# Six column tiles of the input projection in the loop over the cached keys, and two gathers of the cache at the head of the heads' stage

## The chip, the cores and the metric

The kernel runs on one core of a Trainium2 chip. The metric is the device time of one execution in microseconds (us), the median of several runs. The page and the trace shown here come from one more execution, taken with the hardware profiler.

## What is computed

One layer of a hybrid decoder, for a prompt of 512 tokens and for eight sample tokens, each with a cache of 4096 older tokens in 32 pages. All numbers are float32. Cut to what matters:

```python
D_MODEL, SEQ, DEC_BATCH, PAST_LEN, PAGE_SIZE = 1024, 512, 8, 4096, 128
KV_LORA, Q_LORA, MLA_HEADS, MLA_ROPE = 256, 384, 8, 32

z = rmsnorm(h, g_attn) @ w_in            # q|k|v 1536, a 8, b 8, gate z 512, latent q 384, latent kv 256, rotary key 32
q, k, v, g, beta = gdn_prep(causal_conv(ext, w_conv), a, b, a_log, dt_bias)   # conv of 4 taps, silu, l2norm of q and k
o_gdn = gdn_output(gdn_chunked(q, k, v, g, beta)[0], z, g_gdn_out)             # prompt; gdn_recurrent for the samples

q_nope, q_rope, ckv, kr = mla_project(qa, kva, cos, sin, ...)
o_mla = mla_prompt_attention(...)        # prompt: causal attention among its 512 tokens
# samples: every cached page is gathered by page_table, its keys expanded and normed per head
kn_p, v_p = mla_expand(ckv_pool[pages], w_kv_b, g_k_nope)
sc_p = scores(kn_p, kr_pool[pages])      # softmax over 4096 cached tokens and the new one

h = h + concat(o_gdn, o_mla) @ w_o
h = h + (silu(u @ w_ffn_gate) * (u @ w_ffn_up)) @ w_ffn_down        # u = rmsnorm(h, g_ffn)
h = h + (p @ w_ple_proj) * sigmoid(rmsnorm(h, g_ple) @ w_ple_gate)
```

## The kernel before

Every float32 operand of a large product is kept as two float32r parts, hi and lo, and a product is three matmuls, hi*hi, hi*lo and lo*hi. Of a weight, ScalarE (ACT) makes the hi part by a copy and GpSimd (POOL) the lo part by a subtraction (L122, L123). The 520 tokens lie on the free dimension in two halves of 260 columns.

The order of the instructions on each engine is made ahead of time by a scheduler from priorities and its own model of the engines; the program text gives the order in which things are offered to it, and the gathers are offered under a raised priority. On the chip each engine works through its row in order.

The stages are these. Up to 46 us the norm of the tokens and a token-major projection (latent q, latent kv, rotary key, a, b), and the row numbers idx of the gathers. From 46 to 222 us, called the stage of the heads here, two things run side by side. One is the feature-major input projection: 16 column tiles of 128 columns, in `order`, 48 matmuls each into a pair of PSUM banks (ps_in, L664). Tiles 0 to 3 are q, 4 to 7 k, 8 to 11 v, 12 to 15 the gate z. Behind each tile `conv_tail` scales its columns (ct), and for q, k and v makes the convolution (four steps on y by VectorE, DVE), the silu (th by ACT, then a product), four transposes (ps_n), copies and sums of squares; for z it makes the gate and stores it. The other is the generator `latent_heads`, one step (`next(side)`) per k tile: the heads of the latent attention, that is projections of keys, values and queries (ps_k, ps_v, ps_q; ps_q14 is the last one, of the samples in the second half of the heads), their norms (rq, an inverse root by DVE in small steps), the gains (qs and qn by POOL, L578), rotations (rope, L393 to L398), and last, for the samples, the absorbed queries (ps_qg, ps_qabs, ps_qr, tiles qs, sq, qah, bd) that the loop over the keys needs. Its memory is then closed and taken by the pools of the cache (`after_heads`).

The cache comes in 64 groups, eight for a sample, of 512 tokens each. A group is two gathers issued by POOL: raw (512 KB, the latents) and kr (64 KB, the rotary keys). Eleven raw places (NRAW) and twelve kr places (NKR) exist; a raw place comes free when the latents of a sample have been weighted (softmax_pv, `released`), eight groups at a time.

The loop over the cached keys has 256 key tiles of 128 tokens, two for each n. Per pair of key tiles there are four transposes (ps_cT by `latents_T`), a copy (cth) and a subtraction (ctl) for the two parts; per key tile 12 matmuls ps_K (L1368), squares by ACT (sqk), scores by ACT (S), sums by DVE (ssq), and norms, softmax and weighting now and then. After each key tile one step of `filler` is taken (`pace`): the delta rule of the prompt (0.6 of the steps) and the prompt's attention (0.4), then the splits for the output projection, which itself and the FFN follow. TensorE's work up to about 930 us belongs to this loop and its filler; the rest is output projection, FFN and layer embedding.

## Time and profile before

| | us |
|---|---|
| median of 3 runs | 1440.86 |
| lowest and highest run | 1436.94 and 1441.38 |
| span of the profiled execution | 1436.1 |
| TensorE busy in it | 1337.7 (93%) |
| VectorE / ScalarE / GpSimd busy | 849.3 / 572.5 / 642.8 |
| chain of waits: PE / DVE / DMA / another core or an unknown queue | 73% / 12% / 6% / 3% |

The span is the time from the first to the last instruction of the profiled execution; the runs are timed from outside. Busy times are sums of instruction durations. Matmuls overlap one another, so that two of them of 0.28 us each can start 0.12 us apart; rows of a timeline join instructions of one kind that follow each other (x2). PEclk is the clock that TensorE was granted, in parts of its full 2.4 GHz; 0.5 is 1.2 GHz.

### The profile page before, as it was taken

How to read it: one execution, taken by the hardware profiler on the slowest of the kernel's cores; microseconds unless marked ns; L12 is line 12 of the kernel's file. 1: busy time of each engine (PE TensorE's matmuls, PEld its weight loads, DVE VectorE, ACT ScalarE, POOL GpSimd, SP SyncE). 2: the span in 40 equal slices, each digit the busy share in tenths (PEclk: the TensorE clock that was granted, in tenths of full speed). 3: DMA queues.
4: the chain of work that ended last, by engine and by line, in shares of the span. 5: the costliest groups of instructions: out<-in, count | busy, mean ns of one | idle time of the engine just before them, and what ended most of it. 6: DMA issues, size and time to landing. Idle time of an engine off the chain costs nothing.

```text
span 1436.1 us, 27870 instructions
## 1 busy us (share of the span) xinstructions
PE 1337.7 (93%) x11100; PEld 1271.4 (89%) x11100; DVE 849.3 (59%) x1628; ACT 572.5 (40%) x1304; POOL 642.8 (45%) x794
## 2 busy tenths in 40 slices
PE   7998884997898999899999998999999999999998
PEld 6888873996897989799799797989999999999998
DVE  5589991676777765446456575447666665411164
ACT  5354311553464555454355465424222222222232
POOL 3224546354557884321321527336434443445531
PEclk9999987999899999999999999999999999999999
DMA  7434326113454233310400505133333333232331
GB/s 225 108 100 136 67 66 225 28 31 79 155 108 138 59 124 72 119 31 5 136 11 26 168 5 174 39 96 89 91 100 90 89 89 97 88 93 88 94 111 38
DMA packets 198148, 132.41 MB, mean 92 GB/s; under 512 B 65000, under 2 KB 183043, under 8 KB 198012
## 3 DMA queue, kind: packets, MB, share of 16 engines
q1 hardware_dynamic: 186756, 92.88, 24.0%
q0 software_dynamic: 11264, 37.76, 7.8%
q8 instruction: 88, 1.44, 0.4%
q14 instruction: 40, 0.33, 0.1%
HBM read 116.71 MB, written 14.00 MB: 91 GB/s over the span
## 4 chain that ended last, share of the span: by engine, by line
PE 73%; DVE 12%; DMA 6%; another core or an unknown queue 3%; POOL 2%; issue 2%; ACT 1%; SPq 1%; POOLq 0%; DVEq 0%; ACTq 0%
PE ps_K L1368 21%; PE ps_d L1503 9%; PE ps_u L1193 9%; PE ps_g L1193 8%; PE ps_cT L1313 3%; PE ps_pg L1193 3%; PE ps_in L664 2%; DVE y L636 2%; PE ps_wom L1464 1%; PE ps_natA L320 1%; DMA db<-fac_d 1%; PE ps_pv L1284 1%; PE ps_wog L1223 1%; DMA raw<-in_cache_ckv_dram,idx 1%
## 5 line engine op out<-in xcount | busy, mean ns | idle before, releaser
L1368 PE MATMUL ps_K<-wkh,cth 128*128 128x260 f32 x1024 | 229.1, 305 | 8.5 <-issue 5.9
L1373 DVE TENSOR_REDUCE ssq<-sqk 128x8 f32<-128x512 f32 x256 | 174.0, 682 | 104.1 <-ACT sqk L1371 95.8
L1371 ACT ACTIVATE sqk<-ps_K 128x512 f32<-128x512 f32 x256 | 152.6, 597 | 180.0 <-PE ps_K L1368 160.3
L1368 PE MATMUL ps_K<-wkh,ctl 128*128 128x260 f32 x1024 | 214.6, 291 | 1.6 <-issue 1.6
L1368 PE MATMUL ps_K<-wkl,cth 128*128 128x260 f32 x1024 | 214.4, 290 | 0.8 <-issue 0.8
L1368 PEld LDWEIGHTS ps_K<-wkh,cth 128*128 128x128 f32 x1024 | 163.5, 196 | 14.6 <-issue 8.3
L1368 PEld LDWEIGHTS ps_K<-wkl,cth 128*128 128x128 f32 x1024 | 164.3, 195 | 1.9 <-issue 1.6
L1368 PEld LDWEIGHTS ps_K<-wkh,ctl 128*128 128x128 f32 x1024 | 162.6, 194 | 2.6 <-issue 2.0
L1319 DVE TENSOR_TENSOR ctl<-ps_cT,cth 128x512 fp32r<-128x512 f32 x128 | 87.5, 684 | 42.3 <-ACT cth L1318 36.0
L1313 PE MATMUL ps_cT<-cst,raw 128*128 128x128 f32 x512 | 81.8, 282 | 25.3 <-DVE ctl L1319 19.4
L1318 ACT ACTIVATE cth<-ps_cT 128x512 fp32r<-128x512 f32 x128 | 77.1, 603 | 69.0 <-PE ps_cT L1313 31.0
L608 POOL DMA_INDIRECT kr<-in_cache_krope_dram,idx x64 | 63.5, 993 | 83.0 <-PE ps_kr L1240 69.7
L1313 PEld LDWEIGHTS ps_cT<-cst,raw 128*128 128x128 f32 x512 | 60.9, 146 | 30.1 <-DVE ctl L1319 21.1
L123 POOL TENSOR_TENSOR wg_l<-wg_r,wg_h 128x1024 fp32r<-128x1024 f32 x22 | 53.6, 2436 | 71.6 <-ACT wg_h L122 71.6
L123 POOL TENSOR_TENSOR wu_l<-wu_r,wu_h 128x1024 fp32r<-128x1024 f32 x22 | 52.7, 2396 | 66.8 <-ACT wu_h L122 66.8
L123 POOL TENSOR_TENSOR wd_l<-wd_r,wd_h 128x1024 fp32r<-128x1024 f32 (+1 forms) x24 | 53.1, 2211 | 65.8 <-ACT wd_h L122 65.8
L123 POOL TENSOR_TENSOR win_l<-win_r,win_h 128x1024 fp32r<-128x1024 f32 x16 | 38.8, 2431 | 90.7 <-ACT win_h L122 90.7
L606 POOL DMA_INDIRECT raw<-in_cache_ckv_dram,idx x64 | 62.7, 979 | 33.1 <-issue 11.2
L1193 PE MATMUL ps_g<-ul,wg_h 128*128 128x260 f32 x352 | 71.0, 283 | 0.9 <-DVE ul L1432 0.7
L1193 PE MATMUL ps_u<-uh,wu_l 128*128 128x260 f32 x352 | 71.7, 283 | 0.0
L1193 PE MATMUL ps_u<-ul,wu_h 128*128 128x260 f32 x352 | 71.6, 283 | 0.0
L1193 PE MATMUL ps_u<-uh,wu_h 128*128 128x260 f32 x352 | 71.5, 283 | 0.0
(577 smaller groups left out, 3535.1 us busy)
## 6 DMA issues: line engine op xcount, KB each, us to landing
wg_r<-in_w_ffn_gate_dram SPq DMA_DIRECT2D x22, 512.0 KB
wu_r<-in_w_ffn_up_dram SPq DMA_DIRECT2D x22, 512.0 KB
win_r<-in_w_in_dram SPq DMA_DIRECT2D x16, 512.0 KB
wd_r<-in_w_ffn_down_dram SPq DMA_DIRECT2D x16, 512.0 KB
wpg_r<-in_w_ple_gate_dram SPq DMA_DIRECT2D x8, 512.0 KB
db<-fac_d SPq DMA_DIRECT2D x8, 384.0 KB
wd_r<-in_w_ffn_down_dram SPq DMA_DIRECT2D x8, 384.0 KB
xres<-xT_d SPq DMA_DIRECT2D x8, 260.0 KB
```

Source lines behind the costliest of these rows:

```text
L123: gp.tensor_tensor(out=lo, in0=raw, in1=f(hi), op=ALU.subtract)
L606: gp.indirect_dma_start(out=raws[G].rearrange("p t c -> p (t c)"), out_offset=None, in_=ckv_rows, in_offset=off)
L608: gp.indirect_dma_start(out=krs[G], out_offset=None, in_=kr_rows, in_offset=off)
L636: ve.scalar_tensor_tensor(out=y[:, s:], in0=ct[:, :SEQ - s], scalar=wtap(i, j), in1=y[:, s:], op0=ALU.mult, op1=ALU.add)
L1193: te.matmul(o[hf], w[a][:, k, :], mov[b][:, k, hf * HN:(hf + 1) * HN], start=k == 0 and (a, b) == (0, 0), stop=k == K - 1 and a == 1)
L1313: te.transpose(pt[:, (s * 2 + k) * P:(s * 2 + k + 1) * P], raw[:, (n % 2) * 2 + s, k * P:(k + 1) * P], ident)
L1318: sc.activation(hi, p4, AF.Copy)
L1319: ve.tensor_tensor(out=lo, in0=p4, in1=f(hi), op=ALU.subtract)
L1368: te.matmul(pk[:, hf, :260], x[:, s * 2 + k, :], y[:, k, hf, c0:c0 + 260], start=k == 0 and x is cur[0] and y is wkh, stop=k == 1 and x is ...
L1371: sc.activation(sq, pk[:, :, wo:wo + 256], AF.Square)
L1373: ve.tensor_reduce(out=ssq[:, i, :], in_=sq.rearrange("p f (h c) -> p (f h) c", h=4), axis=AX.X, op=ALU.add)
L1503: te.matmul(ps[:, hf, :HN], w[a][:, k, :], (fh, fl)[b][:, q0 + k, hf * HN:(hf + 1) * HN], start=q0 + k == 0 and a + b == 0, stop=q0 + k == ...
```

## The change

Six parts:

1. The loop of the stage of the heads keeps ten tiles, in the order 4, 12, 5, 13, 6, 14, 7, 15, 0, 1. Tiles 2, 3, 8, 9, 10 and 11 are made by a generator `project_qkv`, which stands at the head of the filler of the loop over the keys: four steps a tile (two halves of the columns, each in two halves of k), before the delta rule and the prompt's attention start.
2. Weights of the input projection come in pieces of four k tiles (256 KB) instead of eight (512 KB), with the splits half as long.
3. In the convolution, the copy of the last 11 columns and the first tap go from DVE to ACT, and its steps are taken between the matmuls of the next tile.
4. The gathers of the first two groups are issued at the head of the stage of the heads, into the place of oTm (free until the attention's outputs come) and into a tile kr_early; `after_heads` then issues eleven more. NKR goes from 12 to 11.
5. `pace` grows by 1.1 per key tile instead of 1.0.
6. The activations xh, xl and rb stay until `project_qkv` is done; the pool of the prompt's attention opens then. (Comments are gone as well, so that line numbers differ.)

```diff
-    NRAW, NKR = 11, 12
+    NRAW, NKR = 11, 11
+    early = 2
+    kr_early = dcp.tile([P, early, P], F32, name="kr_early")
     def gathers():
-        while len(raws) < min(NB * 8, NRAW + released[0]):
+        n = early if not dpool else min(NB * 8, NRAW + max(early, released[0]))
+        while len(raws) < n:
             G = len(raws)
-            raws[G] = dpool[1].tile([P, 4, 256], F32, tag="raw", name=f"raw{G}", bufs=NRAW)
-            krs[G] = dpool[1].tile([P, P], F32, tag="kr", name=f"kr{G}", bufs=NKR)
+            if G < early:
+                raws[G] = oTm.rearrange("p j t -> p (j t)")[:, G * 1024:(G + 1) * 1024].rearrange("p (t c) -> p t c", t=4)
+                krs[G] = kr_early[:, G, :]
+            else:
+                raws[G] = dpool[1].tile([P, 4, 256], F32, tag="raw", name=f"raw{G}", bufs=NRAW)
+                krs[G] = dpool[1].tile([P, P], F32, tag="kr", name=f"kr{G}", bufs=NKR)
...
+    def load_win(i):
+        c0 = i * P if i < 12 else CONV + 16 + (i - 12) * P
+        return [load_w(wk, w_in[q * 512:(q + 1) * 512, c0:c0 + P], 4, P, f"win{i}{q}", bufs_raw=2, bufs=3) for q in range(2)]
+
+    def project_qkv(tiles):
+        conv = iter(())
+        for i in tiles:
+            w = load_win(i)
+            ct = cv.tile([P, NT], F32, tag="ct", name=f"ct{i}")
+            for hf in range(2):
+                ps = psf(hf, f"ps_in{i}{hf}")
+                for q in range(2):
+                    for k in range(4):
+                        for a, b in ((0, 0), (0, 1), (1, 0)):
+                            te.matmul(ps[:, :HN], w[q][a][:, k, :], (xh, xl)[b][:, q * 4 + k, hf * HN:(hf + 1) * HN],
+                                      start=q + k + a + b == 0, stop=q + k == 4 and a == 1)
+                    if q:
+                        sl = slice(hf * HN, (hf + 1) * HN)
+                        ve.tensor_tensor(out=ct[:, sl], in0=ps[:, :HN], in1=rb[:, sl], op=ALU.mult)
+                    next(conv, None)
+                    yield
+            for _ in conv:
+                pass
+            conv = convolve(i, ct, psf(0, f"ps_n{i}"))
+        for _ in conv:
+            yield
+
+    def convolve(i, ct, pn):
+        sc.activation(ctail[:, i, :], ct[:, NT - 11:NT], AF.Copy)
         y = cv.tile([P, SEQ], F32, tag="y", name=f"y{i}")
-        ve.tensor_scalar(out=y, in0=ct[:, :SEQ], scalar1=wtap(i, 3), scalar2=None, op0=ALU.mult)
+        sc.activation(y, ct[:, :SEQ], AF.Copy, scale=wtap(i, 3))
...
+    gathers()
     side = latent_heads()
-    order = [4, 5, 6, 7, 0, 1, 2, 3, 8, 9, 12, 10, 13, 11, 14, 15]
-    for i in order:
+    conv = iter(())
+    for i in (4, 12, 5, 13, 6, 14, 7, 15, 0, 1):
...
     def mixers():
+        yield from project_qkv((2, 3, 8, 9, 10, 11))
+        px.close()
+        mhp.append(pmh.enter_context(pool("mh", 2, side="right")))
...
-            pace += 1.0
+            pace += 1.1
```

How this moves instructions is seen at three places. First TensorE at the last q projection. Before, after ps_q14 the next column tile goes on (ps_in12 here; ps_in of six tiles stand behind it in all):

```order
L561 MATMUL ps_q14_1595<-wqb1_h_1506,qaTl_1195 8x384
L561 MATMUL ps_q14_1595<-wqb1_l_1507,qaTh_1194 8x384
L644 MATMUL ps_n8_2006<-cst_133,y8_1998 128x128 x2
L664 MATMUL ps_in12_2090<-xh_95,win12_h_2086 128x260
L664 MATMUL ps_in12_2090<-xl_96,win12_h_2086 128x260 x2
L664 MATMUL ps_in12_2090<-xh_95,win12_l_2087 128x260 x2
```

In the changed kernel, at the same place:

```order
L561 MATMUL ps_q14_1609<-wqb1_h_1519,qaTl_1209 8x384
L561 MATMUL ps_q14_1609<-wqb1_l_1520,qaTh_1208 8x384
L675 MATMUL ps_n1_2029<-cst_133,kq_81 128x128 x4
L1358 MATMUL ps_cT0_2122<-cst_133,oTm_82 128x128 x4
L509 MATMUL ps_qg_1693<-cst_133,sq_1_1686 128x8 x4
L518 MATMUL ps_qabs0_1707<-qgT_1698,wkT_627 128x8 x8
L518 MATMUL ps_qabs1_1720<-qgT_1698,wkT_627 128x8 x8
L532 MATMUL ps_qr_1741<-cst_133,sq_2_1687 128x8 x4
L646 MATMUL ps_in20_2170<-xh_95,win20_h_2159 128x260
```

All ten tiles now stand ahead of ps_q14; behind it come the last transposes of tile 1, the first transposes of the cache, read from oTm, and the absorbed queries, and only then the first matmuls of tile 2 (ps_in20 and ps_in21 are its two halves). After 21 of those the second group of ps_qr follows.

Second TensorE where the loop over the keys begins (cT is the transposed cache, K00 and K01 the first two key tiles). Before:

```order
L664 MATMUL ps_in15_2417<-xh_95,win15_l_2414 128x260 x2
L1313 MATMUL ps_cT0_2499<-cst_133,raw0_1847 128x128 x4
L1368 MATMUL ps_K00_2517<-wkh_99,cth0_2504 128x260 x2
L1368 MATMUL ps_K00_2517<-wkl_100,cth0_2504 128x260 x2
L1368 MATMUL ps_K01_2534<-wkh_99,cth0_2504 128x260 x2
L1368 MATMUL ps_K01_2534<-wkl_100,cth0_2504 128x260 x2
L1313 MATMUL ps_cT1_2508<-cst_133,raw0_1847 128x128 x4
```

In the changed kernel (win30 and win31 are the two halves in k of the weights of tile 3):

```order
L646 MATMUL ps_in21_2239<-xh_95,win21_l_2166 128x260
L646 MATMUL ps_in30_2322<-xh_95,win30_h_2311 128x260
L646 MATMUL ps_in30_2322<-xl_96,win30_h_2311 128x260
L646 MATMUL ps_in30_2322<-xh_95,win30_l_2312 128x260
L1416 MATMUL ps_K00_2140<-wkh_99,cth0_2127 128x260 x2
L1416 MATMUL ps_K00_2140<-wkl_100,cth0_2127 128x260 x2
L1416 MATMUL ps_K01_2183<-wkh_99,cth0_2127 128x260 x2
L1416 MATMUL ps_K01_2183<-wkl_100,cth0_2127 128x260
L1358 MATMUL ps_cT1_2131<-cst_133,oTm_82 128x128 x4
```

Tile 2 and a part of tile 3 now stand ahead of the first key tiles. Behind K01 follow 16 more matmuls of tile 3 and then ps_cT2, which before follows K01 directly.

Third POOL, where weights are split (win_l) and gathers issued. Before, the first gathers stand behind the last split of the stage:

```order
L123 TENSOR_TENSOR win15_l_2414<-win15_r_2411,win15_h_2413 128x1024
L606 DMA raw0_1847<-in_cache_ckv_dram,idx_107 128x1024
L606 DMA raw1_1851<-in_cache_ckv_dram,idx_107 128x1024
L606 DMA raw2_1855<-in_cache_ckv_dram,idx_107 128x1024
L606 DMA raw3_1859<-in_cache_ckv_dram,idx_107 128x1024
```

In the changed kernel, far ahead of that:

```order
L244 TENSOR_TENSOR wA_l_147<-wA1_r_168,wA_h_146 128x1536
L614 DMA oTm_82<-in_cache_ckv_dram,idx_107 128x1024 x2
L616 DMA kr_early_631<-in_cache_krope_dram,idx_107 128x128 x2
L123 TENSOR_TENSOR win40_l_645<-win40_r_642,win40_h_644 128x512
L123 TENSOR_TENSOR win41_l_651<-win41_r_648,win41_h_650 128x512
```

The first two groups are asked for right after the weights of the token-major part are split. Eleven raw (raw2 to raw12) and eleven kr gathers still stand in a row where the heads end, 22 instead of 23; the splits of tile 3's second half and of tile 8 stand behind them.

## Rows read from the trace of the kernel before

**Rows 1.** The page, busy time (share of the span) and instructions of each engine.

```profile
PE 1337.7 (93%) x11100; PEld 1271.4 (89%) x11100; DVE 849.3 (59%) x1628; ACT 572.5 (40%) x1304; POOL 642.8 (45%) x794
```

**Rows 2.** Busy time by stretch: PE, PEld, DVE, ACT, POOL, PEclk, DMA share, GB/s.

```profile
66.00:170.00 104.00, 91.09 (x677) 85.44 (x676) 96.04 (x159) 45.63 (x82) 46.49 (x23) 0.99 0.38 98
170.00:216.00 46.00, 38.95 (x292) 38.08 (x291) 42.12 (x95) 10.20 (x15) 17.09 (x11) 0.87 0.28 81
216.00:252.00 36.00, 14.47 (x92) 14.03 (x91) 5.80 (x11) 4.08 (x9) 21.73 (x23) 0.70 0.67 225
...
324.00:349.00 25.00, 21.76 (x199) 19.63 (x201) 22.00 (x50) 10.93 (x32) 8.41 (x15) 0.93 0.26 54
...
600.00:700.00 100.00, 96.23 (x885) 87.37 (x885) 53.02 (x123) 45.21 (x124) 27.27 (x56) 0.95 0.17 53
```

**Rows 3.** What PE waited for, 46 to 222 us: total, times, longest.

```profile
PE ps_in L664 <- DVE rqs L397: 7.0, 1, 7.0
PE ps_q L561 <- ACT qn L566: 2.0, 1, 2.0
...
PE ps_v L476 <- DVE vs L481: 0.9, 1, 0.9
```

**Rows 4.** Timeline of POOL: start, duration, instruction, idle time before and its end.

```profile
40.25 4.76 POOL L123 TENSOR_TENSOR win_l<-win_r,win_h 128x1024 fp32r<-128x1024 f32 x2 [10.75 <-ACT win_h L122]
...
186.14 3.88 POOL L578 TENSOR_TENSOR qn<-qn,vecs 128x384 f32<-128x384 f32 x4
190.00 4.62 POOL L123 TENSOR_TENSOR win_l<-win_r,win_h 128x1024 fp32r<-128x1024 f32 x2
...
215.89 1.13 POOL L606 DMA_INDIRECT raw<-in_cache_ckv_dram,idx  x1 [8.03 <-DVE S L1260]
...
243.49 0.94 POOL L608 DMA_INDIRECT kr<-in_cache_krope_dram,idx  x1 [0.30 <-issue]
```

**Rows 5.** Timeline of PE, about the last q projection and the loop's start.

```profile
169.73 0.52 PE L561 MATMUL ps_q<-wqb_l,qaTh 128*8 128x384 f32 x1
...
221.57 0.40 PE L664 MATMUL ps_in<-xh,win_l 128*128 128x260 f32 x2
221.80 0.60 PE L1313 MATMUL ps_cT<-cst,raw 128*128 128x128 f32 x4
...
249.98 1.12 PE L1313 MATMUL ps_cT<-cst,raw 128*128 128x128 f32 x4 [15.83 <-DVE ctl L1319]
```

**Rows 6.** The chain of waits, then POOL's timeline, in mid-loop.

```profile
694.84 10.65 another core or an unknown queue
...
704.75 0.94 POOL L606 DMA_INDIRECT raw<-in_cache_ckv_dram,idx  x1 [0.31 <-issue]
```

**Rows 7.** The chain of waits, then PE's timeline, at 349 to 363 us.

```profile
349.12 13.98 DMA raw<-in_cache_ckv_dram,idx
...
359.95 0.59 PE L1295 MATMUL ps_l<-cst,ls 128*128 128x1 f32 x2 [4.39 <-issue]
363.14 1.12 PE L1313 MATMUL ps_cT<-cst,raw 128*128 128x128 f32 x4 [2.61 <-DMA raw<-in_cache_ckv_dram,idx]
```

**Rows 8.** DVE by line, 46 to 216 us: count, busy us, mean ns, idle before.

```profile
L636 DVE SCALAR_TENSOR_TENSOR y<-ct,cols,y 128x511 f32<-128x511 f32 (+2 forms) x36 | 37.3, 1036 | 0.4
L624 DVE TENSOR_TENSOR ct<-ps_in,rb 128x520 f32<-128x520 f32 x14 | 9.6, 689 | 0.9 <-PE ps_in L664 0.8
L633 DVE TENSOR_SCALAR y<-ct,cols 128x512 f32<-128x512 f32 x12 | 7.9, 660 | 0.0
L631 DVE COPY ctail<-ct 128x11 f32<-128x11 f32 x12 | 6.5, 542 | 0.2
```

**Rows 9.** Timeline of DVE in the last third of the stage of the heads.

```profile
189.20 5.50 DVE L396 TENSOR_TENSOR qs<-rqs,rqs 8x64 f32<-8x64 f32 x1
...
195.97 0.73 DVE L636 SCALAR_TENSOR_TENSOR y<-ct,cols,y 128x511 f32<-128x511 f32 x1
...
205.60 3.59 DVE L636 SCALAR_TENSOR_TENSOR y<-ct,cols,y 128x511 f32<-128x511 f32 x2
```

More of the change, by code (lines that the diff above doesn't have):

```diff
@@ L620, in kern @@
     cv = px.enter_context(pool("cv", 2, side="right"))
-    def conv_tail(i, ps):
-        ct = cv.tile([P, NT], F32, tag="ct", name=f"ct{i}")
-        ve.tensor_tensor(out=ct.rearrange("p (a n) -> p a n", a=2), in0=ps[:, :, :HN], in1=rb2, op=ALU.mult)
-        if i >= 12:
-            th = cv.tile([P, NT], F32, tag="th", name=f"thz{i}")
-            sc.activation(th, ct, AF.Tanh, scale=0.5)
-            ve.scalar_tensor_tensor(out=th, in0=th, scalar=1.0, in1=ct, op0=ALU.add, op1=ALU.mult)
-            nc.sync.dma_start(zs_d[:, i - 12, :], th)
-            return
-        ve.tensor_copy(ctail[:, i, :], ct[:, NT - 11:NT])
+    def load_win(i):
[25 more added lines that the diff above has]
+        sc.activation(ctail[:, i, :], ct[:, NT - 11:NT], AF.Copy)
         y = cv.tile([P, SEQ], F32, tag="y", name=f"y{i}")
-        ve.tensor_scalar(out=y, in0=ct[:, :SEQ], scalar1=wtap(i, 3), scalar2=None, op0=ALU.mult)
+        sc.activation(y, ct[:, :SEQ], AF.Copy, scale=wtap(i, 3))
         for j in (2, 1, 0):
@@ L637, in conv_tail @@
                                     op0=ALU.mult, op1=ALU.add)
+            if j == 1:
+                yield
         th = cv.tile([P, NT], F32, tag="th", name=f"th{i}")[:, :SEQ]
         sc.activation(th, y, AF.Tanh)
+        yield
         dst = kq[:, 1 - i // 4, i % 4, :SEQ] if i < 8 else y
         ve.scalar_tensor_tensor(out=dst, in0=th, scalar=1.0, in1=y, op0=ALU.add, op1=ALU.mult)
-        pn = psc(f"ps_n{i}")
         for t in range(4):
@@ L651, in conv_tail @@
             sc.activation(sq, pn, AF.Square)
+            yield
             ve.tensor_reduce(out=(ss_k if i >= 4 else ss_q)[:, :, 2 * j:2 * j + 2],
                              in_=sq.rearrange("p (t h c) -> p t h c", t=4, h=2), axis=AX.X, op=ALU.add)
+        yield
+    gathers()
     side = latent_heads()
-    order = [4, 5, 6, 7, 0, 1, 2, 3, 8, 9, 12, 10, 13, 11, 14, 15]
-    for i in order:
-        c0 = i * P if i < 12 else CONV + 16 + (i - 12) * P
-        w = load_w(wk, w_in[:, c0:c0 + P], 8, P, f"win{i}", bufs_raw=2)
+    conv = iter(())
+    for i in (4, 12, 5, 13, 6, 14, 7, 15, 0, 1):
+        w = load_win(i)
         ps = mm2(f"ps_in{i}")
@@ L663, in kern @@
                 for hf in range(2):
-                    te.matmul(ps[:, hf, :HN], w[a][:, k, :], (xh, xl)[b][:, k, hf * HN:(hf + 1) * HN],
+                    te.matmul(ps[:, hf, :HN], w[k // 4][a][:, k % 4, :], (xh, xl)[b][:, k, hf * HN:(hf + 1) * HN],
                               start=k == 0 and a + b == 0, stop=k == 7 and a == 1)
-            if next(side, side) is side and not dpool:
-                after_heads()
-        conv_tail(i, ps)
+            next(side, None)
+            next(conv, None)
+        ct = cv.tile([P, NT], F32, tag="ct", name=f"ct{i}")
+        ve.tensor_tensor(out=ct.rearrange("p (a n) -> p a n", a=2), in0=ps[:, :, :HN], in1=rb2, op=ALU.mult)
+        if i < 12:
+            for _ in conv:
+                pass
+            conv = convolve(i, ct, psc(f"ps_n{i}"))
+            continue
+        th = cv.tile([P, NT], F32, tag="th", name=f"thz{i}")
+        sc.activation(th, ct, AF.Tanh, scale=0.5)
+        ve.scalar_tensor_tensor(out=th, in0=th, scalar=1.0, in1=ct, op0=ALU.add, op1=ALU.mult)
+        nc.sync.dma_start(zs_d[:, i - 12, :], th)
+    for _ in conv:
+        pass
     for _ in side:
         pass
-    if not dpool:
-        after_heads()
-    px.close()
+    after_heads()
     d0 = dpool[0]
@@ L683, in prompt_heads @@
     def prompt_heads():
+        mh = mhp[0]
         for h in range(8):
@@ L1322, in kern @@
     pmh = ExitStack()
-    mh = pmh.enter_context(pool("mh", 2, side="right"))
+    mhp = []
     def mixers():
+        yield from project_qkv((2, 3, 8, 9, 10, 11))
+        px.close()
+        mhp.append(pmh.enter_context(pool("mh", 2, side="right")))
         two = [[delta_rule(), 0.6, 0.0], [prompt_heads(), 0.4, 0.0]]
```

## The prediction

> **What bounds the kernel now.** I read the page's busy times first, then busy time by stage, then what ends TensorE's idle time, then the chain of waits and the timelines where idle time is long. TensorE (PE) is busy 1337.7 of 1436.1 us [rows 1]: whatever only moves its work gives nothing, and all that can be won is the 98 us in which it stands idle. They lie in three places.
>
> First, the stage of the heads. From 66 to 170 us PE works 91.09 of 104, VectorE (DVE) 96.04; from 170 to 216 it is 38.95 and 42.12 of 46 [rows 2]: DVE sets the pace, and PE keeps up. PE's waits there are ended by DVE in seven of nine rows, the longest for the rotation of the samples' queries (7.0 us, at 188); the other eight, between 2.0 and 0.9 us, lie before 170 us and sum to 12.7 [rows 3].
>
> Second, the turn to the loop over the keys. GpSimd (POOL) issues 23 gathers in a row, from 215.89 to 244.43 [rows 4]; the next transposes of TensorE that need an answer of another engine start at 249.98, after 15.83 us of idle, 34.1 us after the first gather [rows 5]. PE is busy 14.47 of 36 us at a granted clock of 0.70 [rows 2]. The data were not what was missing: the transposes at 221.80 read the first gather [rows 5]. The same is seen in mid-loop: the chain has 10.65 us from "another core or an unknown queue" at 694.84, and the last of eight gathers in that stretch starts at 704.75 and takes 0.94 [rows 6]. I read this as: while POOL issues gathers back to back, TensorE's completions reach the others late, and when the row of gathers is over they come.
>
> Third, inside the loop: 349.12 to 363.10 us the chain waits for a gather (the twelfth, which needs a place of sample 0), with PE idle for 4.39 and 2.61 us [rows 7].
>
> **The change part by part.** *Where the heads end.* The last q projection (ps_q14) ends at 169.73 + 0.52, about 170 [rows 5]. In TensorE's order 487 matmuls of the input projection stand ahead of it before, 480 after: the ten tiles that stay are just those that were done by then, so the six that move are those that filled PE during the rest of the heads, whose chain runs on alone. So I cost the stage in two pieces.
>
> Up to ps_q14, PE's work is the same 91 us, and DVE loses: two whole tiles of convolution (three taps at 1.036, first tap 0.660, tail 0.542, its last two full-width steps at the 0.69 of ct, so 5.7 each), and for six tiles the tail copy and first tap that ScalarE now does (1.2 each, 7.2), against four gates (0.69 each) that come earlier: 11.4 + 7.2 - 2.8 = 15.8 us [rows 8]. That leaves DVE some 80 beside PE's 91. I take 9 of PE's 12.7 us of waits as gone: ps_q14 at 161 (bounds 156, all gone, and 168).
>
> From ps_q14 to the first gather it is 215.89 - 170.25 = 45.6 us before. Convolution and gates of the tiles beyond the tenth take about 15 us of DVE in that stretch: five single taps at 0.73 and a pair at 3.59, nine full-width operations at 0.69, the rest small [rows 9]. One rotation step at 189.20 takes 5.50, to 194.70; POOL's four products of qn end at 190.02 and its two weight splits run from 190.00 to 194.62 [rows 4, 9]. After the change those two splits are not there, so it should end with the products: 4.6 less. Tile 1's last steps come in (1.3), and PE's small products run after long idling, at the low clock (1). 45.6 - 15 - 4.6 + 1.3 + 1 = 28.3, say 29 (26 to 31): between rotation, transposes, absorbed query and its copies every step waits for the one before. First gather at 190 (182 to 199), 26 earlier than now.
>
> A rule speaks against my reading of the 5.50 us as something that shrinks with the splits. The Trainium skill, "SBUF — State Buffer", section "SBUF: two separate sides", says that whichever of a DVE operation with two SBUF inputs and a GpSimd one starts first holds the shared ports for its whole length. By it the wait ends with the one operation under way, not with the third behind it; DVE waited here through the products and both splits. By that rule 4.6 would not be the splits', the stretch 33 and the sum some 4 higher.
>
> *The row of gathers.* It is 22 long instead of 23 (eleven groups, both arrays), 1.25 us less (their spacing, [rows 4]): first gather to the end of the stall 34.1 - 1.25 = 32.9. What PE can do meanwhile is, before, the rest of tile 15, and after, 46 matmuls of tiles 2 and 3; in both the first two key tiles too, then transposes that wait for the same answer (ps_cT2). So the stall ends at 190 + 32.9 = 222.9 instead of 249.98: -27.1.
>
> *Six tiles in the loop.* 288 matmuls and 24 transposes at 0.12 (two start 0.24 apart, [rows 5]) are 37.4. 21 of the matmuls stand among the last steps of the heads and 46 in the stall, both in idle time: 67 x 0.12 = 8.0. 29.4 remain and are paid in the loop, where PE is busy 96.23 of 100 [rows 2]. Against it, idle time of the loop that such ready work may fill: 3.2 us in 324 to 349 [rows 2], where the filler is the delta rule with its round trips to memory; I take 3 (0 to 10). DVE's, ScalarE's and POOL's parts of the six tiles (some 5 us of DVE each) lie beside it: DVE works 53.02 of 100 there.
>
> *Thirteen groups ahead instead of eleven.* The wait at 349 goes; the eight gathers in a row that follow it stay, with a hold-up like that of 694. Of 7.0 us of idle [rows 7] I take 4 (0 to 7).
>
> *Early gathers.* Four, 5 us, in POOL's idle 10.75 us ahead of 40.25 [rows 4]; they cost nothing on POOL, but may hold up TensorE's answers in the token-major part as the other rows do: 2 (0 to 5). Weights in halves: as many bytes on SP's queue in twice the transfers, with TensorE's tiles of 5.8 us to hide them; 0. Pace 1.1 instead of 1.0: the filler ends in the loop either way; 0.
>
> *Sum*: -27.1 + 29.4 - 3 - 4 + 2 = -2.7. Span 1436.1 - 2.7 = 1433.4. The median of the runs is 4.8 above the profiled span, and I keep that: 1438.2.
>
> **The rivals.** *Slower (B): the chain of the heads gives up less.* Its steps are latencies, and with PE idle its clock falls; the row for it is 170 to 216 with PE at 0.87 in mean although it was 85% busy [rows 2]. With ps_q14 at 166 and 34 us behind it the first gather comes at 200, and each us later is paid: 1438 + 10 = 1448. It is slower than now from a first gather at 192.7 on (1440.9). For it: thirty-odd dependent steps; against it: DVE is full there now.
>
> *Faster (C): the row of gathers no longer stops TensorE.* If 249.98 was missing data or full DMA queues (225 GB/s in 216 to 252, [rows 2]), the two early groups and tiles 2 and 3 carry PE through, and some 15 of the 15.83 us go: 1423. Against it: cT1's answer at 694 and here is late with its data long in.
>
> *Faster (D): the loop has room.* PE's weight loads are busy 87.37 of 100 in 600 to 700 [rows 2]. If that is the true load, the remaining 29.4 - 3 go in beside the rest: 1438 - 26 = 1412. The Trainium skill, "Perfetto Trace Analysis", section "Identifying the Most-Contended Engine", holds that weight-load time and not matmul time shows TensorE's headroom; by it D would be the forecast. Against it: each key tile's answers are due within a few us, so the empty 12% are waits at fixed places, which the added work only partly meets.
>
> *Nothing saved at the wait for gathers, delta rule late (E).* The delta rule starts some 25 key tiles later, and its round trips come to lie among the last prompt heads; if they cost as much there and the wait at 349 only moves, -3 and -4 fall away: 1445.
>
> **How the numbers follow.** The forecast A (1438, own range 1430 to 1446) has 0.40; B 0.24, C 0.12, D 0.10, E 0.14. About 0.3%, 4.3 us, is what a measurement of this kernel can tell from no change: 1436.5 to 1445.2. Faster: 0.16 of A, C, D: 0.38. Slower: 0.22 of B, 0.08 of E, 0.03 of A: 0.33. The rest, 0.29, is within. Likeliest is no change that can be measured, and cases of both signs hold most of the chance. The range reaches to 1414, which takes in C and half of D, and to 1454, most of B.
>
> **What would show it.** In the new trace: ps_q14 near 161 and the first of 22 gathers near 190 (B: near 200; if near 178, I am 12 too high). PE idle for some 20 us between; then a stall of TensorE that ends about 5.5 us behind the last gather (C: none). ps_cT<-raw without a wait at the twelfth group (E: a wait of 10 us or more at the fourteenth). Weight loads still near 88% after key tile 30 (D: over 92% in the first 30). The key loop's last ps_K near 930. Wrong would be the whole account if the first gather comes at 190 and the loop still ends 10 us earlier or later.

## The result and the profile after

The changed kernel takes 1453.19 us (median of 6 runs, 1449.87 to 1461.38) against 1441.12 of the kernel before in the same series: ratio 1.0095, 95% interval 1.0065 to 1.0124. It is slower by about 12 us, where I had forecast no change that can be measured.

The span of the profiled execution is 1448.1 us (before 1436.1). The page's busy times, the row that answers to [rows 1]:

```profile
PE 1348.7 (93%) x11100; PEld 1276.4 (88%) x11100; DVE 824.8 (57%) x1610; ACT 583.6 (40%) x1344; POOL 648.3 (45%) x810
```

TensorE (PE) runs the same 11100 matmuls and is busy 11.0 us longer for them; its idle time is what it was (99.4 against 98.4 us). So the 12 us do not show as idle time in the sum: they are matmuls that took longer, by the busy times. Busy time by stretch shows where (start:end, length, then PE, PEld, DVE, ACT, POOL, granted clock of PE, DMA share, GB/s; the kernel after, against [rows 2]):

```profile
160.00:200.00 40.00, 20.19 (x99) 16.96 (x100) 28.47 (x87) 6.10 (x14) 9.87 (x9) 0.53 0.17 53
200.00:232.00 32.00, 18.44 (x103) 14.95 (x101) 6.60 (x12) 5.88 (x14) 23.66 (x24) 0.69 0.63 212
...
272.00:946.00 674.00, 632.27 (x5450) 582.34 (x5450) 423.61 (x957) 330.95 (x909) 315.34 (x607) 0.96 0.29 79
```

The end of the heads now runs with TensorE half idle and its clock near the lower of the two levels (0.5, 1.2 GHz). The timeline of PE in the kernel after (start, duration, instruction, idle time before and its end), against [rows 5]:

```profile
162.28 0.49 PE L561 MATMUL ps_q<-wqb_h,qaTh 128*8 128x384 f32 x1 [4.31 <-ACT qn L566]
...
164.81 0.52 PE L561 MATMUL ps_q<-wqb_l,qaTh 128*8 128x384 f32 x1
170.85 1.12 PE L675 MATMUL ps_n<-cst,kq 128*128 128x128 f32 x4 [5.52 <-DVE kq L673]
...
184.79 0.59 PE L509 MATMUL ps_qg<-cst,sq 8*128 8x8 f32 x4 [11.03 <-DVE sq L506]
185.68 6.17 PE L518 MATMUL ps_qabs<-qgT,wkT 64*128 64x8 f32 x32 [0.30 <-DVE qgT L511]
...
197.16 0.59 PE L532 MATMUL ps_qr<-cst,sq 8*128 8x8 f32 x4
...
231.84 0.80 PE L1416 MATMUL ps_K<-wkh,cth 128*128 128x260 f32 x2 [0.17 <-ACT S L1420]
```

The last q projection ends at 165.3 (170 before). The 32 small matmuls of the absorbed queries take 6.17 us; in the kernel before, beside column tiles and at a high clock, they took 3.31:

```profile
205.22 3.31 PE L518 MATMUL ps_qabs<-qgT,wkT 64*128 64x8 f32 x32
```

GpSimd (POOL) after, against [rows 4]: the first early gather, then the first and the last of the 22 in a row.

```profile
36.14 1.14 POOL L614 DMA_INDIRECT oTm<-in_cache_ckv_dram,idx  x1 [6.61 <-DVE idx L348]
...
199.65 0.99 POOL L614 DMA_INDIRECT raw<-in_cache_ckv_dram,idx  x1 [18.78 <-issue]
...
226.64 0.94 POOL L616 DMA_INDIRECT kr<-in_cache_krope_dram,idx  x1 [0.30 <-issue]
```

The chain of waits after, at three places (start, length, what):

```profile
192.38 4.85 PE ps_in L646 x21
...
210.89 12.33 another core or an unknown queue
...
223.84 7.20 another core or an unknown queue
```

The first of these is the reader's key to the miss: 21 matmuls of tile 2 stand on the chain between the two groups of ps_qr. VectorE (DVE) after, against [rows 9]: the rotation step that took 5.50 us, and the last key tile of the loop (before at 933.3).

```profile
180.03 0.92 DVE L396 TENSOR_TENSOR qs<-rqs,rqs 8x64 f32<-8x64 f32 x1
...
946.32 0.69 DVE L1421 TENSOR_REDUCE ssq<-sqk 128x8 f32<-128x512 f32 x1 [1.24 <-ACT sqk L1419]
```

From the end of the stall to that last key tile it is 714.5 us after (231.84 to 946.32) and 683.3 before (249.98 to 933.26): 31.2 more. What follows the loop is unchanged (502 and 503 us).

### The profile page after: what moved, and what is told of

It reads as the page before. It is cut to its first block, busy times and chain, and to the rows that moved or that the text cites. A ratio compares the mean times of both kernels' runs of the same rounds, so it can differ in the third digit from the quotient of the medians.

```text
span 1448.1 us, 27976 instructions
## 1 busy us (share of the span) xinstructions
PE 1348.7 (93%) x11100; PEld 1276.4 (88%) x11100; DVE 824.8 (57%) x1610; ACT 583.6 (40%) x1344; POOL 648.3 (45%) x810
## 4 chain that ended last, share of the span: by engine, by line
PE 73%; DVE 11%; DMA 5%; issue 4%; another core or an unknown queue 3%; ACT 2%; POOL 2%; SPq 1%; DVEq 0%; POOLq 0%; ACTq 0%
PE ps_K L1416 18%; PE ps_d L1551 9%; PE ps_u L1238 9%; PE ps_g L1238 8%; PE ps_pg L1238 3%; PE ps_cT L1358 3%; PE ps_in L646 2%; PE ps_in L698 2%; DMA db<-fac_d 2%; DVE ssq L1421 2%; PE ps_pv L1329 2%; PE ps_natA L320 1%; PE ps_wom L1512 1%; PE ps_natB L320 1%
## 5 line engine op out<-in xcount | busy, mean ns | idle before, releaser
L123 POOL TENSOR_TENSOR win_l<-win_r,win_h 128x512 fp32r<-128x512 f32 x32 | 42.7, 1339 | 69.1 <-ACT win_h L122 56.5
```

The costliest lines, as they stand in the source:

```text
L123: gp.tensor_tensor(out=lo, in0=raw, in1=f(hi), op=ALU.subtract)
```

## The experiments

The runs come from several chips: on some of them, the result's among them, the kernel before takes 1434 to 1441 us, on two others 1408 to 1409. Every ratio is to the kernel before on the same chip; I call the first kind chips of 1440, the second chips of 1409. A single profiled execution can lie some us from the median of its kernel, that of tiles_back by 11 (1418.78 against 1408.04); where a text rests on spans the medians stand beside.

### Tiles back, two tiles

```diff
-    for i in (4, 12, 5, 13, 6, 14, 7, 15, 0, 1):
+    for i in (4, 5, 6, 7, 0, 1, 2, 3, 8, 9, 12, 10, 13, 11, 14, 15):
...
-            next(side, None)
+            if next(side, side) is side and not dpool:
+                after_heads()
...
-        yield from project_qkv((2, 3, 8, 9, 10, 11))
+        yield from project_qkv(())
```

> The changed kernel with all 16 column tiles back in the stage of the heads, in the order of before; early gathers, weights in halves, copies on ScalarE and pace 1.1 stay. Theory T (the six tiles were the cover of the heads' dependent chain; without them the chain runs alone, at the low clock, and the loop pays the tiles): the loss goes, 1428 to 1440 median, first long row of gathers at 205 to 216 us, TensorE busy over 80% between ps_q14 and it. Rival P (the loss is in the other parts: halves of weights, ScalarE's copies, the early gathers): it stays at 1448 or more. Rival E (the delta rule late in the loop): the loss goes too, so T and E are told apart by the stretch from ps_q14 to the gathers, not by the time.

Measured, on a chip of 1409: 0.9991 (0.9967 to 1.0015). With all sixteen tiles in the stage of the heads and everything else as changed, the whole loss is gone; halves, early gathers, ScalarE's first tap and pace together neither gain nor lose there.

The next kernel has fourteen tiles in the heads' loop (the order of the change, then 2, 3, 8, 9) and `project_qkv((10, 11))`.

> The changed kernel with four of the six tiles (2, 3, 8, 9) back at the end of the stage of the heads, and only 10 and 11 in the loop. Theory T: four tiles, 23 us of TensorE, fill the chain behind ps_q14 (34.3 us with TensorE idle for some 21), so that the first gather of the long row stays at 199 to 206 while the loop pays 23 us less: 1430 to 1438, all of the loss back and more. Rival L (each tile moved costs the same, about 12/6 = 2 us): 1441 + 4 = 1445.

Measured, same chip: 1.0023 (1.0008 to 1.0037), and the first gather at 215.6, where before has it at 215.89 (spread_before, on a chip of 1409, at 215.6): two tiles out of the heads bring the gathers no sooner. The gain that was expected of the first tiles moved did not come. In this kernel, in tiles_back and in fast_tiles and two_again below, the prompt's attention writes over the two early latents before they are weighted, so that sample 0's output is another; the work is the same. In four_moved below, where I expected it too, the latents are weighted first.

### The end of the heads

The second group of ps_qr is offered ahead of its neighbours, so that the 21 matmuls of tile 2 fall behind it:

```diff
             for q in range(2):
+              with tc.high_priority(300):
                 qr4 =
```

> The changed kernel with the copy and the transposes of the samples' rotary queries (ps_qr) at a higher priority: the second ps_qr stands right behind the absorbed queries and no longer behind 21 matmuls of tile 2. Theory T: those 21 lay on the chain (4.85 us at the low clock), so the first gather comes 4 to 6 us earlier, near 194.5, and the time falls by 3 to 6 us, to 1447 to 1450. Rival: the row of gathers and the stall behind it move, but TensorE has that much less to do in the stall, and the time stays at 1453.

Measured, on a chip of 1409: 1.0054 (1.0027 to 1.0081). TensorE in this run, the two groups of ps_qr and the matmuls between them:

```profile
193.84 0.56 PE L533 MATMUL ps_qr<-cst,sq 8*128 8x8 f32 x4 [0.71 <-DVE qgT L511]
194.34 4.03 PE L518 MATMUL ps_qabs<-qgT,wkT 64*128 64x8 f32 x22
198.30 0.59 PE L533 MATMUL ps_qr<-cst,sq 8*128 8x8 f32 x4
```

From ps_q14 to the first gather it is now 30.0 us; in the seven traces with six tiles in the loop and this edit left out it is 33.3 to 34.8. So the 21 matmuls cost about what the chain said. The whole kernel is not measurably better for it: 1.0054 beside the 1.0051 of the change itself (after_again below, on the other chip of 1409). In this execution ps_q14 came at 173, where those seven traces have it at 165 to 170; why is not known, and the 4 us are too few to be seen beside it.

### Early gathers and pace

```diff
-    early = 2
-    kr_early = dcp.tile([P, early, P], F32, name="kr_early")
+    early = 0
...
-    gathers()
     side = latent_heads()
```

> The changed kernel without the two early gathers (twelve kr places, as before): eleven groups are asked for where the heads end, and the twelfth waits for a place of sample 0. Theory T: the early gathers are no part of the loss; without them the wait for a gather of 10 us or more near key tile 44 comes back and the first transposes of the cache stand behind the row of gathers: 1455 to 1466. Rival P: the four gathers at 36 to 41 us hold up the token-major part and cost more than they bring: 1445 to 1452.

Measured, on a chip of 1409: 1.0092 (1.0057 to 1.0127). The change as it is, and the change with the old pace, both on the other chip of 1409:

```diff
-            pace += 1.1
+            pace += 1.0
```

> The changed kernel once more, unchanged, so that it and the other runs of this call stand beside the same runs of before on one chip. Theory T (the six tiles covered the heads' chain; the loop pays them) and its rivals alike expect 1.005 to 1.012 of before here.

> The changed kernel with pace 1.0 instead of 1.1. Theory E (part of the loss is that the delta rule starts some 25 key tiles later, behind the six tiles, and its waits meet less cover): the filler comes later still, and the time rises by 3 to 8 us over that of the unchanged change. Theory T without E: the same work of TensorE in another order, within 3 us.

Measured: after_again 1.0051 (1.0027 to 1.0074), pace1 1.0085 (1.0054 to 1.0117). Neither explains the loss, which is there without either. Pace 1.0 is no better than 1.1; what the early gathers alone are worth cannot be read from this, since the change as it is was not run on the chip of no_early.

### Spreading the row of gathers

Groups are asked for four ahead of the loop, and with a lower priority, instead of eleven at once (in the kernel before and in the changed one):

```diff
+    now = [0]
...
-        while len(raws) < min(NB * 8, NRAW + released[0]):
+        while len(raws) < min(NB * 8, NRAW + released[0], now[0] // 2 + 4):
...
-            with tc.high_priority(1500):
+            with tc.high_priority(200):
...
+        now[0] = n
```

> The kernel before with its gathers spread: four groups (eight gathers) where the heads end, then one group per four key tiles, and a smaller lead in priority. Theory G (while POOL issues gathers back to back, TensorE's completions and instructions come late; no data were missing): the row of 23 gathers shrinks to 8, the stall of 15.8 and 5.7 us to under 8, and the eight-gather stops of the loop lose a part: 10 to 22 us faster than before. Rival D (data and DMA traffic stop TensorE): as many bytes are still wanted by then, 0 to 5 us.

> The changed kernel with its gathers spread in the same way (four groups in all where the heads end, two of them early, so two groups or four gathers in a row). Theory G: TensorE is no longer held up behind the first gather, 8 to 20 us faster than the unchanged change, and TensorE runs the first key tiles and tiles 2 and 3 without its gaps of about one instruction per us. Rival D: 0 to 4 us.

Measured, on the chip of after_again: 1.0003 (0.9984 to 1.0023) and 1.0019 (1.0001 to 1.0037). These say little of the stall, since on this chip there hardly is one. Busy time of after_again in the row of gathers:

```profile
200.00:232.00 32.00, 30.27 (x255) 30.07 (x254) 17.64 (x31) 15.41 (x38) 24.31 (x26) 1.00 0.61 208
```

The same program, the same stretch, the same DMA share (0.61 and 0.63) and GB/s as in the result, and TensorE busy 30.27 of 32 us instead of 18.44. So full DMA queues, the condition of my rival C, are not enough to stop TensorE there; what makes the chips differ I could not try, and it stays open.

### The delta rule sooner

If the loss in the loop is the delta rule's late start, its tiles should be made faster at first:

```diff
-            pace += 1.1
+            pace += 1.1 if n > 6 else 2.2
```

> The changed kernel with pace 2.2 for the first 14 key tiles, so that the six tiles are done by key tile 13 and the delta rule starts some 12 key tiles earlier. Theory E (part of the loss is the late delta rule): 3 to 8 us faster than the changed kernel, 0.999 to 1.003 of before. Theory T without E: within 2 us of the changed kernel, 1.004 to 1.0065.

> The kernel before once more, unchanged, for its trace on the chip of the other runs (all of them some 30 us below the first times, before and changed kernel alike). Theory G1 (on the first chip TensorE is held up behind the row of 23 gathers, on this one hardly): first key tile's sum near 226 us as in the run with spread gathers, and idle time of TensorE between 216 and 252 us under 8 instead of 21.5. Rival: the stall is here too (the sum near 250), and spreading the gathers brought nothing because their number, not their row, counts.

Measured, on a chip of 1440: fast_tiles 1.0126 (1.0095 to 1.0157), no better than the change's 1.0095. The kernel before, a single execution on that chip, took 1442.97, and its stall is there as in the first trace (TensorE busy 14.12 of the 36 us from 216 to 252). Busy time of fast_tiles from the 17th key tile to the last:

```profile
277.00:958.00 681.00, 638.61 (x5479) 590.17 (x5479) 424.37 (x958) 331.49 (x912) 317.03 (x608) 0.95 0.29 81
```

681 us against 674 with the change: idle time and clock are no better. But the edit moved the delta rule little: its first loads (db) start at 344.7 where the change has them at 352.8, and its load of the samples' state (St) at 483.4 against 481.9. So that reading is not borne out, and it is hardly tested either.

### Four tiles

Twelve tiles in the heads' loop, four in the loop over the keys, and the `after_heads` lines of tiles_back:

```diff
-    for i in (4, 12, 5, 13, 6, 14, 7, 15, 0, 1):
+    for i in (4, 12, 5, 13, 6, 14, 7, 15, 0, 1, 2, 3):
...
-        yield from project_qkv((2, 3, 8, 9, 10, 11))
+        yield from project_qkv((8, 9, 10, 11))
```

> The changed kernel with tiles 2 and 3 back at the end of the stage of the heads, and 8 to 11 in the loop; the prompt's attention then overwrites the two early latents before sample 0 has weighted them, so that sample 0's output is another. (That held for the runs with all tiles back and with two moved as well.) Theory T (the heads' chain runs 34 us alone, and what stands beside it is free up to that): the first gather stays at 199 to 203 us, the loop pays 12.4 us less than in the changed kernel: 0.996 to 1.001 of before, better than two moved (1.0023) and six moved (1.0051). Rival L (a straight line, some 0.0009 for each tile moved): 1.0035 to 1.004, the first gather 5 us or more later.

Measured, on the same chip: 0.9918 (0.9887 to 0.9948), faster than the kernel before by 0.8% and better than expected, but not for the reason expected: the first gather comes at 213.8, not at 199 to 203. The same with the gathers spread as above:

> Four tiles moved and the gathers spread (four groups in all at the start, then one per four key tiles). With theory T and the 0.3% that spreading gave the changed kernel: 0.993 to 0.999 of before, faster than both kernels. Rival L: 1.000 to 1.002.

Measured: 1.0066 (1.0044 to 1.0089). Nothing is moved but gathers, and the gain is gone and more. Busy time of four_spread from the 17th key tile to the last, TensorE idle for 42 us of it:

```profile
282.00:943.00 661.00, 619.01 (x5395) 574.66 (x5394) 416.46 (x947) 327.50 (x902) 314.13 (x607) 0.96 0.30 83
```

### How many tiles, on one chip

The same two lines with other tiles: (10, 11), (8, 9, 10, 11) and (3, 8, 9, 10, 11) in the loop over the keys, and the change as it is.

> Two tiles (10, 11) in the loop, the other fourteen in the stage of the heads, to be laid beside four, five and six tiles of the same call. 182 matmuls of tiles then stand between ps_q14 and ps_qg (86 with four, 38 with five, none with six). T (the chain of the heads' end hides tiles up to some number, and what is moved beyond that is paid): time falls from none to the knee and rises behind it, so two is near four, 0.990 to 0.996 of before. P (every tile moved is paid in full in the loop, 6.2 us, and gives back about as much ahead of the first gather; what is left is where the rows of gathers fall in the loop): two is 0.997 to 1.004, and no smooth curve over the number of tiles. The prompt's attention overwrites the two early latents before sample 0's are weighted here, so that sample's output is another; the work is the same.

> Tiles 8 to 11 in the loop, once more, on the chip of the other three. Both T and P: the order of the instructions is the same as in four_moved, so where the row of gathers stops TensorE (before near 1440) it is 0.989 to 0.995 of before again; on a chip where it hardly does (before near 1410) T gives 0.994 to 0.999, P 1.001 to 1.005.

> Tiles 3 and 8 to 11 in the loop, tile 2 back in the stage of the heads. T: half way between four and six, 0.998 to 1.003 of before where before is near 1440, with the first gather 38 matmuls (4.6 us) later than with six, near 204. P: the first gather near 204 as well, but the time is not half way; it may lie outside the two, and the loop from the last gather to the last key tile, 682 us with four and 719 with six, is not near 700.

> The changed kernel again, on the chip of the other three. T and P: 1.005 to 1.010 of before. The loop from the last gather to the last key tile near 719 us where before is near 1440 (678 where it is near 1410).

And on a third chip of 1440, tiles (9, 10, 11) in the loop, and the kernel before with the change's pace alone:

```diff
-            pace += 1.0
+            pace += 1.1
```

> Tiles 9, 10 and 11 in the loop, thirteen tiles in the stage of the heads; 134 matmuls of tiles stand between ps_q14 and ps_qg. So far, on chips where before is near 1440: two 1.0075 of before, four 0.988 and 0.992, five 0.998, six 1.0105. T (a curve with its best place at four): three lies between two and four, 0.994 to 1.002. P (the loop's idle time, set by which step of the filler meets a row of gathers): with 24 to 28 us of TensorE idle between key tile 16 and the last it is 0.987 to 0.994, with 37 to 47 it is 1.000 to 1.009; nothing between is expected. On a chip where before is near 1410: 1.000 to 1.005 by either. If the prompt's attention overwrites the early latents before sample 0's are weighted here, that sample's output is another; the work is the same.

> The kernel before with pace 1.1 instead of 1.0 and nothing else: no tile and no gather is moved, only the filler's steps meet the rows of gathers at other places. T: 0.998 to 1.002 of before, since no work is moved. P: TensorE's idle time between key tile 16 and the last, 38 us in before, changes by 5 us or more, and the time with it by 0.4% or more to one side.

Measured, all on chips of 1440 (times in us; "chain" is the time from the end of ps_q14 to the first gather, and the last two columns are the loop from the 17th key tile to the last, from the rows below):

| tiles in the loop | ratio to before, interval | chain | first gather | loop | TensorE idle in it |
|---|---|---|---|---|---|
| 0, before | 1 | 45.6 | 215.9 | 649 | 38.6 |
| 0, before_pace | 1.0018 (0.9995 to 1.0042) | 46.7 | 217.7 | 653 | 32.4 |
| 2, two_again | 1.0075 (1.0048 to 1.0103) | 51.0 | 216.6 | 663 | 46.3 |
| 3, three_moved | 1.0003 (0.9979 to 1.0026) | 49.6 | 213.7 | 656 | 37.0 |
| 4, four_again | 0.9881 (0.9845 to 0.9917) | 45.0 | 213.6 | 636 | 23.7 |
| 5, five_moved | 0.9979 (0.9955 to 1.0003) | 39.0 | 207.4 | 655 | 37.3 |
| 6, after_third | 1.0105 (1.0051 to 1.0160) | 33.8 | 202.6 | 674 | 41.0 |

The rows of that loop, columns as above (length, then PE busy and its matmuls first, the granted clock third from the end). Before:

```profile
284.00:933.00 649.00, 610.38 (x5310) 563.63 (x5308) 411.72 (x917) 321.63 (x886) 311.16 (x602) 0.97 0.29 82
```

Busy time of before_pace there:

```profile
284.00:937.00 653.00, 620.61 (x5372) 572.96 (x5372) 414.81 (x924) 324.09 (x890) 310.19 (x607) 0.97 0.29 84
```

Busy time of two_again there:

```profile
281.00:944.00 663.00, 616.67 (x5339) 568.97 (x5338) 418.44 (x939) 325.18 (x897) 309.52 (x600) 0.96 0.28 79
```

Busy time of three_moved there:

```profile
281.00:937.00 656.00, 619.02 (x5347) 572.05 (x5347) 412.09 (x939) 325.27 (x897) 308.24 (x601) 0.96 0.29 80
```

Busy time of four_again there:

```profile
287.00:923.00 636.00, 612.26 (x5388) 567.18 (x5387) 412.95 (x947) 326.88 (x900) 313.20 (x604) 0.98 0.30 85
```

Busy time of five_moved there:

```profile
281.00:936.00 655.00, 617.74 (x5398) 573.51 (x5397) 415.28 (x951) 328.44 (x904) 312.49 (x606) 0.97 0.29 81
```

Busy time of after_third there:

```profile
275.00:949.00 674.00, 632.96 (x5448) 582.39 (x5447) 422.77 (x958) 331.29 (x910) 313.62 (x606) 0.96 0.28 79
```

What follows. The four-tile version is repeated on a second chip (0.9918, 0.9881) and beats both kernels: by 0.8 and 1.2% the kernel before, by 2.1% the change (1423.02 against 1453.14 on that chip). Its first gather comes 11 us later than with six tiles, and yet it ends 28 us sooner. Four against six, from the rows: the loop begins 12.3 us later (the sum of key tile 17 starts at 287.3 and 275.0) and is 38 us shorter. 17.3 of the 38 are TensorE's idle time; 60 matmuls less are 7.2 at 0.12; the other 13.5 I put down to the clock, 0.98 instead of 0.96 of some 630 us. By this working idle time in the loop is paid twice, once itself and once in the clock.

Neither theory came through whole. A curve with its best place at four (T) is what three, four, five and six tiles draw, but two, slower than none, is off it. T's reason does not hold either: with no tile put back the chain is 33.8 us, with one 39.0 and with two 45.0, so each costs 5 to 6 us, as much as its 48 matmuls at 0.12 (5.8). They stand ahead of ps_qg, a step of the chain, and are not hidden by it, as P had it. That the idle time is set by what meets the rows of gathers (P) is borne out by four_spread (four tiles, 42 us idle, no gain), but P put two and five elsewhere, and before_pace has 6 us less idle time and no gain: more of the filler went into the loop, 62 matmuls, and the loop is longer by 4.

Where a part of the idle time lies can be shown. TensorE in two_again, behind a row of eight gathers that ends at 438.3:

```profile
441.03 0.64 PE L1418 MATMUL ps_K<-wkl,cth 128*128 128x260 f32 x2
453.60 1.06 PE L740 MATMUL ps_kT<-cst,kn 128*96 128x128 f32 x4 [11.93 <-issue]
```

Busy time there in two_again, and then in the same stretch of four_again, on the same chip, whose row of gathers begins at 435.0:

```profile
441.00:454.00 13.00, 1.07 (x6) 0.79 (x5) 2.11 (x4) 0.00 (x0) 3.21 (x4) 0.50 0.86 197
```

four_again:

```profile
441.00:454.00 13.00, 12.96 (x99) 12.68 (x99) 7.98 (x17) 6.13 (x17) 11.28 (x11) 0.88 0.87 313
```

With the DMA engines equally full, 0.86 and 0.87, nearly the whole core stands in one kernel and works on in the other. So which instructions meet the row decides, not the row alone.

The traces point at one of them, the delta rule's load of St (two transfers of 512 KB). SyncE's queue (SPq) in two_again, where the gathers of raw run from 427.96 to 438.3 (start, time that issuing took, instruction):

```profile
428.48 5.75 SPq L1024 DMA_DIRECT2D St<-in_state_gdn_dram  x2
434.29 13.17 SPq L733 DMA_DIRECT2D vv<-v_d  x1
```

In four_again, where they run from 434.96 to 445.5, it is issued behind them:

```profile
454.30 3.53 SPq L1024 DMA_DIRECT2D St<-in_state_gdn_dram  x2
```

Of the twenty traces four have the load of St beside such a row: two_moved, two_again, three_moved and four_spread. In these TensorE is idle for 12 to 16 of the 26 us from that load on, in the other sixteen for 1 to 6. That fits the loss of two_again and four_spread. But no run moves this load alone, and why the two together stop the core stays open.

## Why the prediction was wrong, point by point

- **What bounds the kernel**: right. TensorE stays at 93%, and what counted was its idle time and its clock.
- **Up to ps_q14**: 165.3, forecast 161 (bounds 156 and 168). VectorE was relieved, by more than I had worked out: some 80 us up to ps_q14, and in the kernel after 69.49 up to 160:

```profile
66.00:160.00 94.00, 87.27 (x656) 83.05 (x655) 69.49 (x125) 46.64 (x93) 45.45 (x30) 1.00 0.44 122
```

  But of TensorE's waits fewer went than the 9 of 12.7 us I took: some 9 are left, the longest 4.31 us for the samples' qn, a wait on the chain of the heads itself.
- **From ps_q14 to the first gather**: the first step that failed. 34.3 us (165.3 to 199.65), forecast 29. The 4.6 us of the rotation step did go (5.50 to 0.92), so the wait did end with POOL's products once no split stood behind them. Before, it began beside the last of the four products (189.20) and lasted through both splits (194.70). The rule of the Trainium skill, "SBUF — State Buffer", section "SBUF: two separate sides", by which I had put the stretch at 33, would have given nearly the right length by the wrong term. What I had wrong: I counted the 21 matmuls of tile 2 "among the last steps of the heads" as lying in idle time. They stand between the two groups of ps_qr, on the chain: 4.85 us. And I gave the low clock 1 us; ps_qabs alone cost 6.17 - 3.31 = 2.9. Together that is 6.8 us above my sum; the stretch is 5.3 above it, so its other terms were some 1.5 too high. qr_first shows the first of these by itself: without the 21 matmuls 30.0.
- **The row of gathers**: the length was right. 199.65 to 231.84 is 32.2 us, forecast 32.9, and as read the stall ends 4.3 us behind the last gather. With both misses it ended at 231.84 instead of 222.9, 8.9 us late. My reading of why, answers that reach the other engines late, is not shown. In the second half of the row TensorE's own matmuls start late, with nothing shown that they wait for:

```profile
221.12 0.57 PE L646 MATMUL ps_in<-xl,win_h 128*128 128x260 f32 x1 [1.04 <-issue]
222.53 0.38 PE L646 MATMUL ps_in<-xh,win_l 128*128 128x260 f32 x1 [0.83 <-issue]
```

  And on the chips of 1409 the same row hardly stops it.
- **Six tiles in the loop**: the sum of the work was met, the idle time was wrong; this is the second step that failed. TensorE is busy 6.9 us longer up to key tile 17 (40.8 us from the stall's end against 33.9), 16.8 for 140 more matmuls behind it and 5.1 by longer matmuls: 28.8, forecast 29.4. That the two agree is in part luck: the matmuls alone are 23.7, some 190 more between the stall's end and the last key tile where I had 245 (29.4 at 0.12), and the rest is the lower clock, which I had not in the sum. And I took 3 + 4 us of idle time as filled or gone, and the loop's idle time rose by some 3 (28.8 and 3 are 0.6 more than the 31.2 above, since the rows begin and end at whole us). The wait at 349 did go, as forecast, but idle time came at the next row. Busy time at the row of gathers of before at 349, and at the next one:

```profile
349.00:366.00 17.00, 8.74 (x84) 5.65 (x77) 6.18 (x17) 2.88 (x7) 11.78 (x14) 0.72 0.69 236
444.00:461.00 17.00, 14.92 (x152) 12.12 (x144) 12.10 (x26) 8.24 (x24) 14.44 (x14) 1.00 0.62 179
```

  The same two rows of gathers after:

```profile
339.00:354.00 15.00, 13.98 (x122) 11.10 (x115) 8.03 (x24) 4.82 (x15) 9.81 (x11) 0.93 0.62 218
437.00:454.00 17.00, 10.20 (x90) 7.00 (x88) 4.91 (x15) 5.54 (x15) 12.91 (x21) 0.71 0.77 280
```

  8.3 us idle becomes 1.0 at the first row, and 2.1 becomes 6.8 at the second, with the clock at 0.71. The filler that stands there has changed; none of this idle time ends with a gather, and its longest piece (4.43 us) ends with ScalarE.
- **Early gathers, halves, pace**: the early gathers lie in POOL's idle time at 36 us as forecast, and I charged 2 us that I cannot find; tiles_back has all of these edits together and costs nothing.
- **The sum**: 8.9 for the later end of the stall, 8.8 for the loop (31.2 instead of 22.4), 1.1 less behind it and 2 less for the early gathers give 14.6 of the 14.7 us between the span forecast, 1433.4, and 1448.1.
- **The rivals**: B met the numbers (ps_q14 at 166, 34 us, first gather at 200), and its falling clock is a part of the miss, but it had not the 21 matmuls and priced the loop as I did. E's 7 us were lost as well, but not by its signs: no wait of 10 us stands at the fourteenth group, and its late delta rule is not borne out by fast_tiles, which hardly tested it. I had the two as alternatives, and their prices add: 1438 + 10 + 7 = 1455. D did not come: weight loads are busy 582 of 674 us, 86%, and the tiles were paid in full. The rule of the Trainium skill, "Perfetto Trace Analysis", section "Identifying the Most-Contended Engine", that the weight-load time shows the headroom, would have given D. C did not come on this chip; on the chips of 1409 the row hardly stops TensorE in most kernels, and the change is slower there too.

## What to carry to other kernels

Before moving ready work away from a chain of dependent steps, follow the chain instruction by instruction in the new order. Count each filler instruction that stands ahead of a chain step as paid: here 21 matmuls cost the chain 4 to 5 us, and one column tile put back 5 to 6. Count the chain's own small matmuls at the low clock where nothing is left beside them (6.17 us instead of 3.31). Then vary how much is moved, and look at what the new order lays beside each row of transfers: six tiles lost 1% and four gained 1%, and most of the difference between them lies in the later loop, not in the chain on which I had spent my working.

## What was not expected of the hardware

- While GpSimd issues 22 gathers in a row TensorE started about one instruction a us in the row's second half on one chip (18.44 us busy of the 32) and ran on nearly untouched on another (30.27 of 32), in the same program at the same DMA share.
- Behind a row of eight gathers the whole core stood for some 12 us in one order of the filler (TensorE 1.07 us busy of 13) and not at all in another (12.96), with the DMA engines at 0.86 and 0.87. In four traces of twenty a load of 1 MB (St) was issued beside such a row: TensorE was idle for 12 to 16 of the next 26 us in these, for 1 to 6 behind that load in the others.
- The granted clock: 0.53 over 40 us in which TensorE was half idle, and 32 small dependent matmuls took 6.17 us there instead of 3.31.
